# Moving a block transpose's transfers to SyncE and letting another planner order the body, in a hybrid mLSTM and DeltaNet decoder block

## The chip, the cores and the metric

The kernel runs on one core of a Trainium2 chip. A core has TensorE (matmul), VectorE, ScalarE, GpSimd and SyncE, each with its own queue of instructions that it works off in order, and 16 DMA engines that all queues share. SyncE and ScalarE issue the transfers here. The metric is the device time of one execution in microseconds; beside it stands the span of the profiled execution, from its first to its last recorded instruction.

## The reference

One layer over 512 tokens of width 2048, in float32:

```
u    = rmsnorm(x, norm_w)
proj = u @ w_in                                  # some 20,500 columns
mLSTM branch (8 heads, q and k of 128, v of 256):
    chunkwise matrix memory with exponential input gate, sigmoid forget gate, running maximum
    h_a = rmsnorm(h_a) * ml_norm_w * sigmoid(ml_o) * silu(ml_z)
DeltaNet branch (16 heads of 128):
    q, k, v = silu(causal conv of width 4); q, k L2-normalised
    delta rule in chunked WY form: (I + tril(b k k^T decay, -1)) sol = rhs, then a recurrence
    h_b = rmsnorm(h_b, dn_norm_w) * silu(dn_z)
y    = sigmoid(gate_a) * (h_a @ w_out[:2048]) + sigmoid(gate_b) * (h_b @ w_out[2048:])
out  = rmsnorm(x + y, final_norm_w)
```

The kernel uses chunks of 128 tokens, which gives the same function.

## The kernel before

**Products.** The float32 products are made of three fp32r products each: a weight tile `wr` (256 KB, loaded by SyncE at L146) is split into a rounded part `wh` (ScalarE, `split_hi`, L113) and a rest `wl` (VectorE, `split_lo`, L116), and `u` was split in the same way into `uh` and `ul`. `proj_cm` (L212 to L214) makes 256 columns with the channels on the partitions, `proj_wide` (L242 to L244) 512 columns with the tokens on the partitions. Each of the 768 weight tiles feeds twelve matmuls of 128x512. There are four raw buffers (`NRAW`), four pairs of split ones (`NSPL`), and loads are written down up to four tiles ahead of use (`RAHEAD`), splits three (`SAHEAD`).

**Units and steps.** The body goes through twelve units, in rounds of one mLSTM unit (two heads) and two DeltaNet units (two heads each). A unit makes its projections one after the other, and its other work runs as generators beside the projections of later units: `start(gen, wait)` puts one on a list, and `tick()`, called after every six matmuls of a projection, moves each one on whose waiting steps are over. `yield n` means: go on n steps later. So a step is six matmuls.

**A DeltaNet unit.** `dn_front_k` forms k k^T and solves the 32x32 diagonal blocks of the triangular system by substitution on VectorE: 31 pairs of small operations on `tmp` and `xi` (L553, L555). The result goes to DRAM and back in another layout (`xd`, then `tt`, both issued by SyncE), and VectorE transposes `tt` to `tn` (L565). `dn_front_q` makes q k^T (`pqk`, L573), which needs the convolved q in `kq` (L440 to L447: ScalarE copies the projection out of its bank, VectorE convolves, ScalarE takes a tanh, VectorE finishes at L447). `dn_back` (L602 to L636) joins the blocks to the full inverse and uses `tn` and `tt`; `dn_chain` runs the recurrence over four chunks.

**Turned tiles.** `turn` transposes a tile of 128 x (4 x 128) values: VectorE transposes its 32x32 blocks (L468), and `travel` brings the blocks to their places through DRAM, with four writes of 64 KB (L476), one for each quarter of the partitions, and one read of 256 KB (L478). This is done 72 times: for k of the mLSTM heads (`kw`), q (`qn`) and v (`vt`) of the DeltaNet heads, and the normalised results of both (`mhn`, `os`). After a result was turned, `gated` multiplies it with its gate on VectorE and stores it to `h_d` (L482 to L484); it is started `TURN` steps after the turn.

**What sets the order.** TensorE's instructions stay in the order in which they are written (`manual_schedule` for PE). [...] Weight loads and splits are moved forward by `2 * PRIO`, evictions under `urgent()` by `PRIO`, and the four writes under `urgent(2)` by `2 * PRIO`; the read is not moved. [...]

After the units come the merge gates' projections (tanh of them goes to `tg_d`), then the output projection (L937 to L939) with the loads of `h_d`, and the final norm.

Of the kernel before, what the change touches and what calls it, by code (L numbers as in the profile page):

```python
# [17 lines left out]
NC = S // P  # L18
# [8 lines left out]
GNARROW = 4  # L27
GLAG = 3
KLAST = 4
TURN = 9  # L30
KWAIT, QWAIT = 4, 8
EPS = 1e-6
CAP = 15.0
# [6 lines left out]
BS = 32  # L40
# [5 lines left out]


@with_exitstack
def hybrid_block(
    ctx: ExitStack,  # L50
    tc: tile.TileContext,
    x: bass.AP,
# [13 lines left out]
    nc = tc.nc  # L66
# [102 lines left out]
    def urgent(level=1):  # L169
        return tc.high_priority(offset=level * PRIO)  # L170
# [4 lines left out]
    def start(gen, wait=0):  # L175
        active.append([gen, clock["t"] + wait])
# [251 lines left out]
    def row_bcast(r, name):  # L428
        t = wk.tile([P, NC, P], F32, tag="rb", name=name, bufs=3)
        nc.sync.dma_start(t.rearrange("p c t -> p (c t)"), rows_d[r, :].partition_broadcast(P))  # L430
        return t

    def bc(col, n):
        return col.unsqueeze(2).to_broadcast([P, NC, n])
# [22 lines left out]
    def token_norms(pk, dst):  # L457

        jk = wk.tile([P, P], F32, tag="jk", name="njk", bufs=1)
        for c in range(NC):  # L460
            with urgent():
                A.activation(jk, pk[:, c, :], AF.Square, accum_out=dst[:, c:c + 1])

    def turn(src, dst):


        o = dst if dst is not src else wk.tile([P, NC, P], F32, tag="to", name="to", bufs=2)
        V.transpose(o if len(src.shape) == 3 else o.rearrange("p n c -> p (n c)"), src)  # L468
        start(travel(o, dst), 1)

    def travel(o, dst):
        d = dr.tile([16, BS, 4, BS], F32, tag="td", name="td", bufs=8)
        ov = o.rearrange("p n (j c) -> p (n j) c", c=BS)
        with urgent(2):
            for a in range(4):
                nc.scalar.dma_start(d[:, :, a, :].rearrange("m r c -> r m c"), ov[a * BS:(a + 1) * BS])  # L476
        yield 3
        nc.scalar.dma_start(dst, d.rearrange("(n j) r a c -> (j r) n (a c)", n=NC))  # L478
        yield 1

    def gated(hn, w, g, kt):
        V.scalar_tensor_tensor(out=g, in0=hn.rearrange("p c t -> p (c t)"), scalar=w, in1=g, op0=ALU.mult,  # L482
                               op1=ALU.mult)
        nc.sync.dma_start(h_d[kt], g)  # L484
        yield 1

    def dn_front_k(hs, kq, u):
        for j in range(2):
            h = hs[j]
            rb = row_bcast(16 + h, "gb")  # L490
            dm = wk.tile([P, NC, P], F32, tag="dm", name="dm")
            G.affine_select(out=dm, in_=rb, pattern=[[0, NC], [1, P]], channel_multiplier=-1, base=0,
                            compare_op=ALU.is_ge, fill=-1e30)
            A.activation(rb, rb, AF.Exp)
            ge = wk.tile([P, NC], F32, tag="ge", name="ge", bufs=4)
            V.tensor_copy(ge, rb[:, :, P - 1])
            for c in range(NC):
                A.activation(dm[:, c, :], dm[:, c, :], AF.Exp, bias=ngam[:, c, h:h + 1])
            u["dm"].append((dm, rb, ge))
        nk = wk.tile([P, 2, NC], F32, tag="nk", name="nk")  # L500
        cs = wk.tile([P, 2, NC], F32, tag="cs", name="cs")
        for j in range(2):
            pk = psw.tile([P, NC, P], F32, tag="wk", name="pkt")
            for c in range(NC):
                T.transpose(pk[:, c, :], kq[j][:, 0, c * P:(c + 1) * P], ident)
            token_norms(pk, nk[:, j, :])
            ke = wk.tile([P, NC, P], F32, tag="ke", name="ke", bufs=4)
            with urgent():
                A.copy(ke, pk)
            u["ke"].append(ke)  # L510
            yield 1
        V.tensor_scalar(out=nk, in0=nk, scalar1=EPS, scalar2=None, op0=ALU.add)
        V.reciprocal(cs, nk)
        for j in range(2):
            V.tensor_tensor(out=cs[:, j, :], in0=cs[:, j, :], in1=beta[:, :, hs[j]], op=ALU.mult)
        u["nk"] = nk

        for j in range(2):
            dm, eg, ge = u["dm"][j]
            G.tensor_tensor(out=dm, in0=dm, in1=bc(cs[:, j, :], P), op=ALU.mult)  # L520
            ke = u["ke"][j]
            G.tensor_tensor(out=ke, in0=ke, in1=bc(dm[:, :, P - 1], P), op=ALU.mult)
        G.tensor_tensor(out=nk, in0=nk, in1=half, op=ALU.pow)
        yield 3
        ld = dr.tile([2 * NC, 4, BS, BS], F32, tag="ld", name="ld", bufs=2)
        for j in range(2):
            aq = wk.tile([P, NC, 2, P], F32, tag="aq", name="aq", bufs=4)
            u["aq"].append(aq)
            pk = psw.tile([P, NC, P], F32, tag="wk", name="pk")
            for c in range(NC):  # L530
                tsl = slice(c * P, (c + 1) * P)
                T.matmul(pk[:, c, :], kq[j][:, 0, tsl], kq[j][:, 0, tsl], start=True, stop=True)
            with urgent():
                V.tensor_tensor(out=aq[:, :, 0, :], in0=pk, in1=u["dm"][j][0], op=ALU.mult)
            for b in range(4):
                bs = slice(b * BS, (b + 1) * BS)
                nc.sync.dma_start(ld[j * NC:(j + 1) * NC, b, :, :].rearrange("c s t -> s c t"), aq[bs, :, 0, bs])
            yield 1


        ls = wk.tile([P, BS, BS], F32, tag="ls", name="ls", bufs=1)
        for q in range(4):
            nc.sync.dma_start(ls[q * NSYS:(q + 1) * NSYS], ld.rearrange("g b s t -> (g b) s t"))
        xi = wk.tile([P, BS // 4, BS], F32, tag="xi", name="xi", bufs=1)
        G.memset(xi, 0.0)
        for q in range(4):
            G.memset(xi.rearrange("p m t -> p (m t)")[q * NSYS:(q + 1) * NSYS, q:(BS // 4) * BS:BS + 4], 1.0)
        yield 4
        for i in range(BS - 1):
            n, m = BS - 1 - i, i // 4 + 1  # L550
            tmp = wk.tile([P, 80], F32, tag="tmp", name="tmp")
            tv = tmp[:, 0:n * m].rearrange("p (a b) -> p a b", b=n)
            V.tensor_tensor(out=tv, in0=ls[:, i, i + 1:BS].unsqueeze(1).to_broadcast([P, m, n]),  # L553
                            in1=xi[:, 0:m, i].unsqueeze(2).to_broadcast([P, m, n]), op=ALU.mult)
            V.tensor_tensor(out=xi[:, 0:m, i + 1:BS], in0=xi[:, 0:m, i + 1:BS], in1=tv, op=ALU.subtract)  # L555
            if i % 2:
                yield 1
        xd = dr.tile([2 * NC, 4, BS // 4, 4, BS], F32, tag="xd", name="xd", bufs=2)
        tt = wk.tile([P, 2 * NC, BS], F32, tag="tt", name="tt", bufs=1)
        tn = wk.tile([P, 2 * NC, BS], F32, tag="tn", name="tn", bufs=1)  # L560
        with urgent():
            for q in range(4):
                nc.sync.dma_start(xd[:, :, :, q, :].rearrange("g b m t -> (g b) m t"), xi[q * NSYS:(q + 1) * NSYS])
            nc.sync.dma_start(tt, xd.rearrange("g b m q t -> (b m q) g t"))
            V.transpose(tn.rearrange("p g m -> p (g m)"), tt.rearrange("p g t -> p (g t)"))  # L565
        u.update(tn=tn, tt=tt)

# [72 lines left out]
    def dn_chain(j, hs, kq, u):  # L640
# [50 lines left out]
        with urgent():  # L691
            V.tensor_tensor(out=os_, in0=po, in1=bc(rsd, P), op=ALU.mult)
        turn(os_, os_)
        start(gated(os_, normc[:, 32:33], u["g"][j], KT + h), TURN)

# [100 lines left out]
    def ml_fin(j, hs, u):  # L796
        h = hs[j]
        hm = u["hm"][j]
        for i in range(2):
            hn = wk.tile([P, NC, P], F32, tag="os", name="mhn")  # L800
            turn(hm[i], hn)
            kt = 2 * h + i
            start(gated(hn, normc[:, 16 + kt:17 + kt], u["g"][j][i], kt), TURN)
            yield 1
# [168 lines left out]
        nc.sync.dma_start(out[c * P:(c + 1) * P, HD:D], hf[:, c, HD:D])  # L973


# [1 line left out]
_INS = ["x", "norm_w", "w_in", "ml_i_bias", "ml_f_bias", "ml_norm_w", "dn_conv_w",  # L977
        "dn_a_log", "dn_dt_bias", "dn_norm_w", "w_out", "final_norm_w"]
# [20 lines left out]
```

## Time and profile before

| | |
|---|---|
| median of 3 runs | 2459.25 us (2456.11 to 2459.51) |
| profiled execution, its own time | 2458.59 us |
| its span | 2456.8 us |
| mean granted TensorE clock | 0.978 |
| TensorE busy | 2328.6 us, 95% |
| VectorE busy | 1130.9 us, 46% |
| ScalarE busy | 819.9 us, 33%, issuing transfers not counted |
| transfers issued by ScalarE, all kinds | 363 |
| transfers issued by SyncE | 1103 |
| HBM read and written | 260.58 and 42.01 MB |

In the profile PE is TensorE's matmul side and PEld its weight loads, DVE is VectorE, ACT ScalarE, POOL GpSimd and SP SyncE; ACTq and SPq are what those two queues issue. L476 is line 476 of the kernel. `td<-to` means that `td` is written from `to`. A wait "A <- B" is idle time of A's engine ended by B. Busy shares are averages over stages; what one wait is worth is read where it occurs.

### The profile page before, as it was taken

What the parts mean: (1) busy time and instruction counts of PE and PEld (TensorE: products, weight loads), DVE (VectorE), ACT (ScalarE), POOL (GpSimd) and SP (SyncE); (2) the same over time, 40 slices, a digit from 0 to 9 for tenths busy, and PEclk for the clock granted to TensorE, in tenths of its full rate; (3) what the DMA queues carried; (4) which work ended last, traced back from release to release, by engine and by line L of the source; (5) the groups of instructions that cost most, each with busy time, mean ns of one, the idle gap of its engine ahead of it and who ended that gap; (6) DMA issues with size and microseconds to landing.
All of it is one profiled execution on the core that took longest, in us unless ns stands there. A gap on an engine that the chain in (4) does not pass through costs nothing.

```text
span 2456.8 us, 32123 instructions
## 1 busy us (share of the span) xinstructions
PE 2328.6 (95%) x11711; PEld 1941.0 (79%) x11711; DVE 1130.9 (46%) x2187; ACT 819.9 (33%) x1846; POOL 192.6 (8%) x261
## 2 busy tenths in 40 slices
PE   7999987999998799999989999988999999999998
PEld 5888776888877687887768788776998888888886
DVE  5533756433375643238463324747333322433434
ACT  5333342332434233243423324342233322422222
POOL 0000202000020200002020001101000000010010
PEclk9999998999999899999989999998999999999999
DMA  4433544453354445335454533544475443643433
GB/s 146 130 99 96 125 126 113 121 132 95 99 127 121 123 112 133 95 95 136 115 130 108 129 95 96 128 114 114 112 218 168 136 145 112 198 129 115 131 113 128
DMA packets 423199, 304.71 MB, mean 124 GB/s; under 512 B 200065, under 2 KB 362082, under 8 KB 423042
## 3 DMA queue, kind: packets, MB, share of 16 engines
q1 hardware_dynamic: 232898, 264.84, 37.6%
q10 hardware_dynamic: 190144, 37.84, 7.8%
q8 instruction: 91, 1.49, 0.2%
q14 instruction: 66, 0.54, 0.1%
HBM read 260.58 MB, written 42.01 MB: 123 GB/s over the span
## 4 chain that ended last, share of the span: by engine, by line
PE 81%; DVE 9%; DMA 3%; ACTq 2%; issue 2%; ACT 1%; POOL 1%; SPq 0%; DVEq 0%; POOLq 0%
PE pj L212 13%; PE pj L214 13%; PE pj L213 13%; PE py L939 5%; PE py L937 5%; PE py L938 5%; PE pg L243 4%; PE pg L242 4%; PE pg L244 4%; PE pv L242 2%; PE pv L244 2%; PE pv L243 2%; ACTq L476 2%; DVE tmp L553 2%; DVE wl L116 2%; DVE xi L555 2%
## 5 line engine op out<-in xcount | busy, mean ns | idle before, releaser
L116 DVE TENSOR_TENSOR wl<-wr,wh 128x512 fp32r<-128x512 f32 x768 | 533.2, 702 | 949.4 <-ACT wh L113 934.9
L113 ACT CAST wh<-wr 128x512 fp32r<-128x512 f32 x768 | 472.0, 621 | 1357.1 <-PE pj L213 518.9
L212 PE MATMUL pj<-uh,wh 128*128 128x512 f32 x1792 | 739.7, 413 | 32.7 <-ACT thz L454 26.2
L214 PE MATMUL pj<-uh,wl 128*128 128x512 f32 x1792 | 708.6, 395 | 3.8 <-DVE wl L116 3.8
L213 PE MATMUL pj<-ul,wh 128*128 128x512 f32 x1792 | 708.2, 395 | 0.0
L212 PEld LDWEIGHTS pj<-uh,wh 128*128 128x128 f32 x1792 | 343.4, 192 | 102.5 <-ACT thz L454 27.9
L214 PEld LDWEIGHTS pj<-uh,wl 128*128 128x128 f32 x1792 | 341.8, 191 | 82.0 <-DVE wl L116 6.9
L213 PEld LDWEIGHTS pj<-ul,wh 128*128 128x128 f32 x1792 | 343.2, 192 | 64.5
L937 PE MATMUL py<-wh,hh 128*128 128x512 f32 x512 | 199.2, 389 | 0.0
L938 PE MATMUL py<-wl,hh 128*128 128x512 f32 x512 | 199.2, 389 | 0.0
L939 PE MATMUL py<-wh,hl 128*128 128x512 f32 x512 | 199.2, 389 | 0.0
L242 PE MATMUL pg<-wh,uh 128*128 128x512 f32 x384 | 149.4, 389 | 0.0
L243 PE MATMUL pg<-wl,uh 128*128 128x512 f32 x384 | 149.4, 389 | 0.0
L244 PE MATMUL pg<-wh,ul 128*128 128x512 f32 x384 | 149.4, 389 | 0.0
L938 PEld LDWEIGHTS py<-wl,hh 128*128 128x128 f32 x512 | 96.1, 188 | 20.1
L939 PEld LDWEIGHTS py<-wh,hl 128*128 128x128 f32 x512 | 96.1, 188 | 20.0
L937 PEld LDWEIGHTS py<-wh,hh 128*128 128x128 f32 x512 | 96.1, 188 | 19.8
L242 PE MATMUL pv<-wh,uh 128*128 128x512 f32 x256 | 99.6, 389 | 0.0
L243 PE MATMUL pv<-wl,uh 128*128 128x512 f32 x256 | 99.6, 389 | 0.0
L244 PE MATMUL pv<-wh,ul 128*128 128x512 f32 x256 | 99.6, 389 | 0.0
L242 PEld LDWEIGHTS pg<-wh,uh 128*128 128x128 f32 x384 | 72.1, 188 | 15.1
L244 PEld LDWEIGHTS pg<-wh,ul 128*128 128x128 f32 x384 | 72.1, 188 | 15.0
(244 smaller groups left out, 2348.6 us busy)
## 6 DMA issues: line engine op xcount, KB each, us to landing
wr<-in_w_in_dram SPq DMA_DIRECT2D x640, 256.0 KB, 2.8
wr<-in_w_out_dram SPq DMA_DIRECT2D x128, 256.0 KB, 3.0
td<-to ACTq DMA_DIRECT2D x128, 64.0 KB, 2.1
hr<-h_d SPq DMA_DIRECT2D x32, 256.0 KB, 3.6
tgl<-tg_d SPq DMA_DIRECT2D x32, 256.0 KB, 3.1
tg_d<-tgw SPq DMA_DIRECT2D x24, 256.0 KB, 3.7
xt<-in_x_dram SPq DMA_DIRECT2D x8, 512.0 KB, 8.6
gb<-rows_d SPq DMA_DIRECT2D x16, 256.0 KB, 3.9
```

Source lines behind the costliest of these rows:

```text
L113: A.copy(hi, src)
L116: V.tensor_tensor(out=lo, in0=src, in1=hi.bitcast(F32), op=ALU.subtract)
L212: T.matmul(ps[j], hi[:, k, wsl], uh[:, kt, :], start=(kt == 0), stop=False)
L213: T.matmul(ps[j], hi[:, k, wsl], ul[:, kt, :], start=False, stop=False)
L214: T.matmul(ps[j], lo[:, k, wsl], uh[:, kt, :], start=False, stop=(kt == KT - 1))
L242: T.matmul(ps[c], uh[:, kt, tsl], hi[:, 0, :], start=(kt == 0), stop=False)
L243: T.matmul(ps[c], uh[:, kt, tsl], lo[:, 0, :], start=False, stop=False)
L244: T.matmul(ps[c], ul[:, kt, tsl], hi[:, 0, :], start=False, stop=(kt == KT - 1))
L476: nc.scalar.dma_start(d[:, :, a, :].rearrange("m r c -> r m c"), ov[a * BS:(a + 1) * BS])
L937: T.matmul(ps[c], hh[base][:, kt, tsl], hi[:, 0, :], start=(kt == 0), stop=False)
L938: T.matmul(ps[c], hh[base][:, kt, tsl], lo[:, 0, :], start=False, stop=False)
L939: T.matmul(ps[c], hl[base][:, kt, tsl], hi[:, 0, :], start=False, stop=(kt == KT - 1))
```

## The change

Four things change. The transfers of `travel` are issued by SyncE in place of ScalarE. Their steps move: the writes two steps after the turn instead of one, the read four steps after the writes instead of three and with the priority that the writes have, `gated` twelve steps after the turn instead of nine. The VectorE transpose of `tt` to `tn` comes ten steps after its transfers instead of right behind them. And the whole body stands in one `tc.block`, for which the planner takes the framework's timeline simulation as its model of the chip in place of its usual one; so the order of every queue but TensorE's can become another.

```diff
-TURN = 9
+TURN = 12
...
 @with_exitstack
-def hybrid_block(
+def hybrid_body(
...
         V.transpose(o if len(src.shape) == 3 else o.rearrange("p n c -> p (n c)"), src)
-        start(travel(o, dst), 1)
+        start(travel(o, dst), 2)
...
         with urgent(2):
             for a in range(4):
-                nc.scalar.dma_start(d[:, :, a, :].rearrange("m r c -> r m c"), ov[a * BS:(a + 1) * BS])
-        yield 3
-        nc.scalar.dma_start(dst, d.rearrange("(n j) r a c -> (j r) n (a c)", n=NC))
+                nc.sync.dma_start(d[:, :, a, :].rearrange("m r c -> r m c"), ov[a * BS:(a + 1) * BS])
+        yield 4
+        with urgent(2):
+            nc.sync.dma_start(dst, d.rearrange("(n j) r a c -> (j r) n (a c)", n=NC))
         yield 1
...
             nc.sync.dma_start(tt, xd.rearrange("g b m q t -> (b m q) g t"))
+        yield 10
+        with urgent():
             V.transpose(tn.rearrange("p g m -> p (g m)"), tt.rearrange("p g t -> p (g t)"))
...
+def hybrid_block(tc, *args):
+    with tc.block(schedule_with_timeline_sim=True):
+        hybrid_body(tc, *args)
```

## The prediction, made before the changed kernel was run

> **What bounds the kernel now.** I read the page's first two parts, then the list of what TensorE waited for, then the timeline around its long waits, and last the clock in short windows and the page's list of DMA queues.
>
> ```profile
> span 2456.8 us, 32123 instructions
> PE 2328.6 (95%) x11711; PEld 1941.0 (79%) x11711; DVE 1130.9 (46%) x2187; ACT 819.9 (33%) x1846; POOL 192.6 (8%) x261
> ...
> PEclk9999998999999899999989999998999999999999
> ```
>
> TensorE is busy for 95%, so at most 2456.8 - 2328.6 = 128.2 us of idle time, and what a low clock adds, can be won. Where it idles (waits in us in total, times, longest):
>
> ```profile
> PE pqk L573 <- DVE kq L447: 62.3, 8, 11.5
> PE pj L212 <- ACT thz L454: 26.2, 4, 7.0
> PE pprm L103 <- DMA nrow<-in_ml_norm_w_dram: 15.3, 1, 15.3
> PE pj L212 <- ACT wh L113: 5.4, 4, 1.9
> PE pj L214 <- DVE wl L116: 3.8, 3, 1.6
> ```
>
> The 15.3 us are the start, which the change leaves alone. The other four rows, with one wait of 1.1 us on a convolution input, are 98.8 us in the body. They come in rounds of one mLSTM and two DeltaNet units, four rounds in all: each has a short pqk wait (4.1 to 4.4 us), a thz wait (6.1 to 7.0) and a long pqk wait (11.1 to 11.5). Round one in the timeline (start, length, engine, and in brackets the idle time before and what ended it):
>
> ```profile
> 321.53 1.98 ACTq L476 DMA_DIRECT2D td<-to  x4
> ...
> 323.55 5.03 ACTq L476 DMA_DIRECT2D td<-mhn  x8
> 328.62 0.62 ACT L113 CAST wh<-wr 128x512 fp32r<-128x512 f32 x1 [9.04 <-DMA td<-mhn]
> ...
> 330.27 0.79 PE L212 MATMUL pj<-uh,wh 128*128 128x512 f32 x1 [7.05 <-ACT thz L454]
> ...
> 402.63 0.63 ACT L446 ACTIVATE th<-kq 128x512 f32<-128x512 f32 x1
> ...
> 413.61 0.68 DVE L447 SCALAR_TENSOR_TENSOR kq<-th,kq 128x512 f32<-128x512 f32 x1
> ...
> 414.35 2.08 PE L573 MATMUL pqk<-kq 128*128 128x128 f32 x8 [11.55 <-DVE kq L447]
> ...
> 425.22 1.66 ACT L113 CAST wh<-wr 128x512 fp32r<-128x512 f32 x3 [18.06 <-DMA td<-to]
> 428.21 0.45 DVE L565 STREAM_TRANSPOSE tn<-tt 128x256 f32<-128x256 f32 x1 [7.48 <-DMA tt<-xd]
> ```
>
> At 321.5 ScalarE issues twelve writes of turned tiles, from 321.53 to 328.58, and stands 9 us before its next cast; the evictions that free TensorE's banks are behind them. That is the thz wait. At 402.63 the tanh that kq needs starts, so kq could run at 403.3; VectorE's order puts the substitution pairs (L553, L555) first, and kq runs at 413.6. That is the long pqk wait, and it is a matter of order alone.
>
> After a wait TensorE also runs slowly (columns: stretch, its length, PE busy and matmuls, granted clock, DMA share, GB/s):
>
> ```profile
> 331.00:332.00 1.00, 1.00 (x4) 0.50 1.05 309
> ...
> 334.00:336.00 2.00, 2.00 (x11) 1.00 0.69 179
> ```
>
> At clock 0.50 matmuls start 0.43 us apart, at 1.00 0.23. The slow stretch after the return lasts about 3.4 us after a short pqk, 3.6 after a thz and 4.9 after a long pqk wait; half of that is lost: 1.7, 1.8 and 2.4 us.
>
> **The change, part by part.** Round by round, all that waits cost is 62.3 + 4 x (1.7 + 2.4) = 78.7 us for pqk, 26.2 + 4 x 1.8 = 33.4 for thz, 10.3 for the small ones: 122.4. With none of them and nothing new the span would be 2334.
>
> *ScalarE loses the transfers.* 72 turned tiles, each four writes and a read:
>
> ```profile
> L476 ACTq DMA_DIRECT2D td<-to x128: 309/516/1819, 312.3 to 1799.2; - x128
> ...
> L478 ACTq DMA_DIRECT2D mhn<-td x16: 366/383/460, 268.3 to 1615.2; - x16
> ```
>
> 288 writes at 0.51 us and 72 reads at 0.38 us are 147 + 27 = 174 us of ScalarE's queue. Most lay beside matmuls. On the path are the bursts: the four thz waits (33.4 us), and the four waits for a cast (5.4), of which the one at 521.7 follows a burst of 16 writes (511.45 to 521.02). With the writes gone ScalarE goes on to its cast and eviction as soon as the matmuls end, so I take both as won: 38.8 us. Late next would be the banks themselves, at their ordinary 0.6 us evictions. The bounds are 0 (SyncE's burst then stops the weights instead) and 38.8.
>
> *SyncE gains them.* Its 1103 issues take 422 us (summed over its row in the trace) and get 174 more: 596 of 2457. The length is no issue; the place is. Behind a turned tile's write or read on SyncE stand weight loads, the reads of broadcast rows and the h stores; for the weight loads wait ScalarE's cast, VectorE's subtraction and then TensorE. A write now waits for VectorE's transpose, a read for its writes to land (2.1 us median for a write). The cover is the lead of the weights: pairing the n-th load with the n-th tile's first matmul in the trace gives a median of 17.7 us (one in a hundred under 9.7), which agrees with up to four raw and three split tiles ahead of the one in use, 2.72 us each. A burst of twelve writes is 7 us, a wait for landing some 2 us: under the cover. So I cost it at 0; without the cover each such burst would cost up to its 7 us. The long end is ScalarE's stand of 18.06 us above, which is as long as the lead: if SyncE stood so, nothing would be left.
>
> Weight loads and turned tiles have used different rings so far:
>
> ```profile
> q1 hardware_dynamic: 232898, 264.84, 37.6%
> q10 hardware_dynamic: 190144, 37.84, 7.8%
> ```
>
> 7.8% of the span over 72 tiles is 2.7 us of all 16 engines for each tile. Behind one on the same ring a weight load would land in 2.8 + 2.7 = 5.5 us, behind three in 11. The first is well under the lead and the second is not, if SyncE's own stand is added. [...]
>
> *Four steps to the read, two to the writes, TURN 12.* A step is six matmuls, 6 x 0.227 = 1.36 us. Writes come one step later, the read two steps later (1 + 3 steps after the turn, 5.4 us, become 2 + 4, 8.2 us), and the gated product six steps after the read in place of five. VectorE's waits for these reads (vt 15.6, gz 7.4, mg 2.3 us in total) ended no TensorE wait, so 0; tiles are held some 4 us longer, which only a full buffer would show. The read becomes urgent as well, so that it may pass weight loads on SyncE: 0.38 us each, in the cover.
>
> *The transpose of tt waits ten steps.* Now VectorE stands 41.4 us in eight waits for tt. Behind it are weight subtractions; the three waits for wl (3.8 us, one at 429.28 just after the transpose at 428.21) come of it. Gain 3.8. tn is first used 31 us after it was made (304.9 and 336.3), ten steps are 13.6 us, so nobody waits for it: 0; if that cover went, TensorE would wait at L602.
>
> *The order is made anew.* One block ordered by another time model: every order but TensorE's, which is written out, can change. The trace can't show the new one. It can win the 78.7 us of pqk waits, by putting kq before the substitution, or lose: a further group of matmuls in each DeltaNet unit that waits as the long pqk does would cost 8 x (11.4 + 2.4) = 110 us. I take half of the pqk time, 39 us: the four short ones of the eight show the same work at a third of the price, and the tanh of the long one stood 2.3 us behind the turned tiles' writes (its input ended at 400.3), which are gone from that queue. Against it I set new waits of 3 us a round, between the small ones (0.6 to 1.9) and the short pqk: 12 us. Entering and leaving a block is not in the trace; bounds are 0 and 5 us (some twice the longest unexplained stretch in the chain, 2.2 us near the end), taken 1, by the 1.8 us that lie around the span.
>
> Sum: 2456.8 - 38.8 - 3.8 - 39 + 12 + 1 = 2388 for the span. The profiled execution took 2458.6 for its 2456.8, and the median of the runs is 2459.25: add 2.4, so 2391. Within 0.2% (5 us) is what a measurement of this kernel can't tell from no change.
>
> **The rivals.** *Only ScalarE's relief counts*: the new order is as good as the old, and the pqk waits stay. 2459 - 38.8 - 3.8 + 1 = 2418. For it: kq's lateness is VectorE's own affair. Against: the order is made afresh by other times, so that it stays equal would be chance.
>
> *SyncE's line stops the weights*: a write waits there for a late VectorE transpose, loads stand behind it and behind the small packets. ScalarE's waits for td are 138 us in 20 places (61.8 + 65.7 + 6.7 + 3.9); if half of it came through, 69, plus 20 us of slow clock in as many places, less the 42.6 won: 2459 + 69 + 20 - 42.6 = 2505. It decides when SyncE's stand and the landing together pass the lead of 17.7 us. Against it: SyncE waits 1390 us for VectorE to free a raw tile, so it is mostly idle.
>
> *The new order makes another group late*, the case on the other side with one place: a product of the DeltaNet units whose VectorE input is put behind the substitution as kq is. 2459 + 110 - 42.6 + 1 = 2527. From 42 us in total, that is 5 us a unit, it outweighs what ScalarE's relief gives.
>
> *No difference*: thz and casts are held up by other work of ScalarE, and the order comes out alike: 2459.
>
> **How the numbers follow.** Forecast 0.50 (its own range 2340 to 2425: from nearly all 122 us won, to new waits of 45 in place of 12), ScalarE's relief alone 0.15, no difference 0.04, SyncE's line 0.11, the order worse 0.20. Faster 0.65, same 0.04, slower 0.31. The low end, 2340, is just above 2337, all waits gone. The high end, 2510, takes in half of SyncE's line and a third of the bad order (which spreads from 2470 to 2600); left out are 0.05 + 0.13 above and 0.01 below.
>
> **What would show it.** Right: no wait of L212 for thz; td issues in SyncE's row; no ScalarE cast that waits for td; tn without a wait for tt; fewer and shorter pqk waits; ScalarE's busy time unchanged at 820. Wrong: casts that wait for wr landings, TensorE waiting for wh or wl (SyncE's line), or a new row of TensorE waits for a VectorE or ScalarE result of more than 40 us in total (the order), with more 0.50 in the clock.

## The result and the profile after

The changed kernel takes 2416.0 us (median of 4 runs, 2413.2 to 2416.8) beside 2457.7 us before: a ratio of 0.9829 (95% interval 0.9812 to 0.9846). That is 41.7 us faster, where 68 had been forecast (2459 to 2391). The top of its page:

```profile
span 2415.0 us, 32146 instructions
## 1 busy us (share of the span) xinstructions
PE 2318.6 (96%) x11711; PEld 1934.3 (80%) x11711; DVE 1112.4 (46%) x2187; ACT 828.4 (34%) x1846; POOL 188.0 (8%) x261
...
q1 hardware_dynamic: 422978, 302.62, 46.1%
```

The span fell by 41.8 us. TensorE's busy time fell by 10.0 us (2328.6 to 2318.6) for the same 11711 matmuls, because less of it ran at the low clock (mean 0.978, now 0.986). Its idle time fell by 31.8 us (128.2 to 96.4). All turned tiles now travel on SyncE's ring, q1, which carries 302.62 MB in place of 264.84. What TensorE waited for in the changed kernel (total, times, longest):

```profile
PE p L605 <- DVE tn L568: 40.1, 7, 9.9
PE pprm L103 <- DMA nrow<-in_ml_norm_w_dram: 15.8, 1, 15.8
PE pj L212 <- ACT yp L440: 13.0, 8, 4.0
PE pnum L768 <- DVE c L778: 5.9, 4, 1.8
PE put L291 <- DVE xt L284: 5.6, 1, 5.6
PE pj L212 <- ACT thz L454: 4.2, 3, 2.3
PE pqk L576 <- DVE kq L447: 0.4, 1, 0.4
```

The list is turned over. The pqk wait is gone (62.3 us before, 0.4 now), and so, nearly, is the thz wait (26.2, now 4.2) and that for `wh` (5.4, now none). In their place stands a wait that the old profile did not have at all: the first matmuls of `dn_back` (L605) wait 40.1 us for `tn`, seven times in eight units. In the body all waits together were 98.8 us and are 63.6; at the start 4 us were lost (15.3 + 2.1 before, 15.8 + 5.6 now).

The chain to the first of the `tn` waits, from the timeline of all engines in the changed kernel:

```profile
324.01 0.69 DVE L639 TENSOR_TENSOR vt<-vt,nk 128x512 f32<-128x512 f32 x1 [2.71 <-DMA vt<-td]
...
324.82 0.17 DVE L556 TENSOR_TENSOR xi<-xi,tmp 128x8 f32<-128x8 f32 x1
...
326.65 1.01 SPq L146 DMA_DIRECT2D wr<-in_w_in_dram  x2
327.70 2.63 SPq L564 DMA_DIRECT2D xd<-xi  x4
...
332.87 0.37 SPq L565 DMA_DIRECT2D tt<-xd  x1
...
336.07 0.45 DVE L568 STREAM_TRANSPOSE tn<-tt 128x256 f32<-128x256 f32 x1 [2.89 <-DMA tt<-xd]
```

The last pair of the substitution is done at 325.0, having stood on VectorE behind a product that waited 2.7 us for a turned tile; SyncE then issues weight loads and two reads of turned tiles before `xd`, which goes out 2.7 us later (so in every other unit; in the rest, and before the change, `xd` goes out at once); `xd` and `tt` take until 336.0, and `tn` follows at once. Before the change the same unit had its last pair at 297.4 and `tn` at 304.9. The step from the first pair to the last is what grew: 24.0 us on average over the eight units before, 48.8 after. Why, a stretch of VectorE's row in the changed kernel shows:

```profile
302.55 0.22 DVE L556 TENSOR_TENSOR xi<-xi,tmp 128x66 f32<-128x66 f32 x1
302.68 0.75 DVE L443 SCALAR_TENSOR_TENSOR vt<-yp,convc,vt 128x512 f32<-128x512 f32 x1
303.35 0.21 DVE L554 TENSOR_TENSOR tmp<-ls,xi 128x60 f32<-128x60 f32 x1
303.48 0.68 DVE L116 TENSOR_TENSOR wl<-wr,wh 128x512 fp32r<-128x512 f32 x1
304.08 0.75 DVE L443 SCALAR_TENSOR_TENSOR vt<-yp,convc,vt 128x512 f32<-128x512 f32 x1
304.74 0.21 DVE L556 TENSOR_TENSOR xi<-xi,tmp 128x60 f32<-128x60 f32 x1
```

The small operations depend on each other, and the new order lays one or two operations of 0.7 us between them. Counted in the traces, a unit's substitution had 12.5 other VectorE operations inside it before and has 51.0 now. Of the 24.8 us by which it grew 5.9 are waits of VectorE inside it, nearly all for turned tiles (0.3 us a unit before, 6.2 now); the rest is the work laid between. `pqk` was freed by where `kq` now stands: of the 62 small operations 25 or 44 stood ahead of the second `kq` of q before, 3 or 13 now.

### The profile page after: what moved, and what is told of

Its sections match the earlier page's. It is cut to its first block, busy times and chain, and to the rows that moved or that the text cites. A ratio compares the mean times of both kernels' runs of the same rounds, so it can differ in the third digit from the quotient of the medians.

```text
span 2415.0 us, 32146 instructions
## 1 busy us (share of the span) xinstructions
PE 2318.6 (96%) x11711; PEld 1934.3 (80%) x11711; DVE 1112.4 (46%) x2187; ACT 828.4 (34%) x1846; POOL 188.0 (8%) x261
## 3 DMA queue, kind: packets, MB, share of 16 engines
q1 hardware_dynamic: 422978, 302.62, 46.1%
## 4 chain that ended last, share of the span: by engine, by line
PE 81%; DMA 6%; DVE 5%; SPq 4%; ACT 2%; issue 1%; POOL 0%; DVEq 0%; POOLq 0%; ACTq 0%
PE pj L212 13%; PE pj L213 13%; PE pj L214 13%; PE py L940 5%; PE py L942 5%; PE py L941 5%; PE pg L243 4%; PE pg L244 4%; PE pg L242 4%; SPq L476 2%; PE pv L243 2%; PE pv L242 2%; PE pv L244 2%; PE pjt L227 1%; PE pjt L229 1%
## 5 line engine op out<-in xcount | busy, mean ns | idle before, releaser
L116 DVE TENSOR_TENSOR wl<-wr,wh 128x512 fp32r<-128x512 f32 x768 | 539.8, 705 | 879.8 <-ACT wh L113 870.0
L243 PEld LDWEIGHTS pg<-wl,uh 128*128 128x128 f32 x384 | 72.1, 188 | 15.0
```

The source lines that it names most:

```text
L116: V.tensor_tensor(out=lo, in0=src, in1=hi.bitcast(F32), op=ALU.subtract)
L243: T.matmul(ps[c], uh[:, kt, tsl], lo[:, 0, :], start=False, stop=False)
```

## The experiments

Three suspects were to be told apart for the new wait: the new order (which draws out the substitution), SyncE's line (which issues `xd`, `tt` and the turned tiles late), and the ten steps. And the gain had to be divided between the new order and the move to SyncE.

### The parts alone

The order alone is the kernel before with the block around its body.

```diff
-def hybrid_block(
+def hybrid_body(
...
+def hybrid_block(tc, *args):
+    with tc.block(schedule_with_timeline_sim=True):
+        hybrid_body(tc, *args)
```

> The kernel before with its body in the block that is ordered by the timeline simulation; transfers, steps and the transpose of tt stay as before. Theory (the new order removes the pqk waits by putting kq ahead of the substitution, and pays with a late tn, because the substitution is drawn out on VectorE): pqk waits under 5 us in total, substitution some 45 us long in place of 22 to 26, tn waits of 30 to 45 us, thz waits kept at 15 to 30 as ScalarE still issues the bursts; time 2415 to 2440. Rival A (tn is late because SyncE's line holds the xd and tt transfers behind the turned tiles): tn waits under 10 us, time near 2400. Rival B (the ten steps make tn late): the same, tn waits under 10 us.

Measured 2405.5 us, ratio 0.9792 (0.9777 to 0.9806): faster than the whole change. Its waits of TensorE:

```profile
PE p L602 <- DVE tn L565: 18.4, 6, 5.5
...
PE pj L212 <- ACT thz L454: 14.5, 7, 3.8
PE pj L212 <- ACT wh L113: 12.7, 6, 3.0
...
PE pqk L573 <- DVE kq L447: 0.6, 1, 0.6
```

So the order alone takes away the pqk wait and brings the `tn` wait, as the theory had it, with a substitution of 46.9 us. But there are only 18 us of `tn` waits in place of 30 to 45, and the time is under the range given: something else in the change makes `tn` later and costs time.

The rest of the change without the block:

```diff
-def hybrid_block(tc, *args):
-    with tc.block(schedule_with_timeline_sim=True):
-        hybrid_body(tc, *args)
```

> The changed kernel without the block, so with the order of the usual planner: SyncE issues the turned tiles, with the new steps and the ten steps for tn. Theory: thz waits and casts behind td writes gone (under 5 us), pqk waits kept at 40 to 62 us, substitution 22 to 26 us long and no tn wait; time 2415 to 2430. Rival A (SyncE's line): tn waits of 20 us or more here too. Rival B (ten steps): tn waits here too.

Measured 2550.0 us, ratio 1.0382 (1.0367 to 1.0398), so 93 us slower than before, where 27 to 42 faster was expected. TensorE's waits in it (total, times, longest):

```profile
PE p L605 <- DVE tn L568: 81.0, 8, 16.7
PE pj L212 <- ACT wh L113: 45.1, 8, 10.2
PE pj L212 <- ACT thz L454: 39.4, 4, 10.6
...
PE pqk L576 <- DVE kq L447: 4.7, 4, 1.2
```

SyncE's row of the timeline around the first substitution in the same run (start, us, what it issued, how many):

```profile
285.60 0.46 SPq L544 DMA_DIRECT2D ls<-ld  x1
297.80 3.44 SPq L146 DMA_DIRECT2D wr<-in_w_in_dram  x4
301.49 6.47 SPq L476 DMA_DIRECT2D td<-to  x8
...
319.24 2.80 SPq L146 DMA_DIRECT2D wr<-in_w_in_dram  x3
322.09 1.40 SPq L544 DMA_DIRECT2D ls<-ld  x3
```

One of the four reads of `ls` is issued at 285.6; the other three stand behind weight loads, the next of which goes out 12 us later, and behind sixteen writes of turned tiles, until 322.1. The substitution starts at 327 and `tn` comes at 351. So it is in four of the eight units. In the other four the reads are in time, but the `xd` writes go out 14 to 26 us after the last pair, with weight loads before them, and `tn` starts 31 to 33 us after it (6.5 to 7.9 before). ScalarE, too, stood longer for weights (casts that waited for `wr`: 69.4 us, 30.9 before). SyncE's line is late here, as in the rival of that name, but the transfers that stand in it to TensorE's cost are the substitution's own, which the rival did not name; the next run shows how much of the time they are.

The list shows another thing that was not expected: the pqk waits are 4.7 us in place of 62.3, under the usual planner. Given other steps and another issuer, it too lays down another order: 0 or 10 of the small operations stand ahead of the second `kq` of q here. So the block is not the only way to free `kq`.

To see whether the place in SyncE's line is the cause, the small transfers were moved forward:

```diff
-                nc.sync.dma_start(ld[j * NC:(j + 1) * NC, b, :, :].rearrange("c s t -> s c t"), aq[bs, :, 0, bs])
+                with urgent(2):
+                    nc.sync.dma_start(ld[j * NC:(j + 1) * NC, b, :, :].rearrange("c s t -> s c t"), aq[bs, :, 0, bs])
...
-            nc.sync.dma_start(ls[q * NSYS:(q + 1) * NSYS], ld.rearrange("g b s t -> (g b) s t"))
+            with urgent(2):
+                nc.sync.dma_start(ls[q * NSYS:(q + 1) * NSYS], ld.rearrange("g b s t -> (g b) s t"))
...
-        with urgent():
+        with urgent(2):
             for q in range(4):
                 nc.sync.dma_start(xd[:, :, :, q, :].rearrange("g b m t -> (g b) m t"), xi[q * NSYS:(q + 1) * NSYS])
```

> The run e2_sync_alone (the change without the new order) with the small transfers of the substitution (ld, ls, xd, tt) moved forward in the priority as far as the weight loads and the turned tiles. Theory (in e2 the three ls reads stand on SyncE behind weight loads that wait for a free buffer and behind sixteen writes, so that the substitution starts 41 us after the first of them): first ls read to first substitution pair under 12 us, tn waits under 20 us in place of 81, time 2430 to 2490. Rival (the lateness is not one of SyncE's order): tn waits stay over 50 us, time over 2520.

Measured 2463.3 us, ratio 1.0022 (1.0013 to 1.0031). The first `ls` read is 6.1 us ahead of the first pair, and the `tn` wait is gone from the list of TensorE's waits:

```profile
PE pj L212 <- ACT wh L113: 55.6, 15, 10.2
PE pj L214 <- DVE wl L116: 33.1, 7, 6.7
...
PE pqk L578 <- DVE kq L447: 4.7, 4, 1.2
```

So 87 of the 93 us hung on where a few small transfers stand on SyncE. What is left are 88.7 us of waits for `wh` and `wl`. Casts still wait 53.2 us for `wr`, but the longest of TensorE's waits are not late weights. Of the waits for `wh` four of about 10 us make up 39.7; before the first of them ScalarE's row shows

```profile
424.44 0.63 ACT L446 ACTIVATE th<-vt 128x512 f32<-128x512 f32 x1 [3.61 <-DVE vt L443]
...
427.00 1.12 ACT L113 CAST wh<-wr 128x512 fp32r<-128x512 f32 x2
```

The weight tile of that cast had landed at 419.3; the cast stood behind a tanh whose input VectorE made between pairs of the substitution, and behind the squares of q that follow it. Of the waits for `wl` four of 6.2 to 6.7 us make up 25.3, and in these the subtraction comes 7.7 us after its cast, behind an unbroken stretch of the substitution. So under the usual planner the rest of the change wins nothing even so: the pqk waits have gone, and others have taken over, 65 us of them from where the substitution stands on VectorE.

The converse: the whole change with ScalarE issuing the turned tiles again.

```diff
-                nc.sync.dma_start(d[:, :, a, :].rearrange("m r c -> r m c"), ov[a * BS:(a + 1) * BS])
+                nc.scalar.dma_start(d[:, :, a, :].rearrange("m r c -> r m c"), ov[a * BS:(a + 1) * BS])
...
-            nc.sync.dma_start(dst, d.rearrange("(n j) r a c -> (j r) n (a c)", n=NC))
+            nc.scalar.dma_start(dst, d.rearrange("(n j) r a c -> (j r) n (a c)", n=NC))
```

> The changed kernel with the turned tiles' transfers issued by ScalarE again, all else kept (steps, block, ten steps). Theory: tn waits stay at 30 us or more, as the substitution is still drawn out; thz waits come back with the bursts, 10 to 30 us; time 2425 to 2450. Rival A (SyncE's line): tn waits fall under 15 us; time under 2410.

Measured 2403.9 us, ratio 0.9783 (0.9768 to 0.9797). TensorE's waits in this run:

```profile
PE pj L212 <- ACT wh L113: 23.1, 7, 5.9
PE pj L212 <- ACT thz L454: 17.8, 4, 5.2
```

There is no `tn` wait in this list, against the theory, which wanted 30 us or more; rival A had it right. The bursts on ScalarE are back with 40.9 us of waits, and still the kernel is 12 us faster than the changed one. So SyncE's part in the changed kernel swaps 41 us of waits for `thz` and `wh` against 59 of others (`tn` 40.1, `yp` 13.0, `pnum` 5.9). With the new order alone, which differs from this run in the steps, the time was the same (2405.5), with 18.4 us of `tn` waits: where ScalarE issues, the steps are worth nothing that can be told from zero.

The block itself, with the usual planner, which lays down the same order as before:

```diff
-    with tc.block(schedule_with_timeline_sim=True):
+    with tc.block():
```

> The kernel before in a plain block with the usual planner; every queue has the same instructions in the same order as before. This prices entering and leaving the block: theory 0 to 5 us, so 2457 to 2462.

Measured 2458.5 us over 10 runs, ratio 1.0003 (0.9994 to 1.0013): no cost that can be told from zero.

### What makes tn late

First the substitution itself, moved forward in the priority:

```diff
-            V.tensor_tensor(out=tv, in0=ls[:, i, i + 1:BS].unsqueeze(1).to_broadcast([P, m, n]),
+            with urgent():
+                V.tensor_tensor(out=tv, in0=ls[:, i, i + 1:BS].unsqueeze(1).to_broadcast([P, m, n]),
...
-            V.tensor_tensor(out=xi[:, 0:m, i + 1:BS], in0=xi[:, 0:m, i + 1:BS], in1=tv, op=ALU.subtract)
+                V.tensor_tensor(out=xi[:, 0:m, i + 1:BS], in0=xi[:, 0:m, i + 1:BS], in1=tv, op=ALU.subtract)
```

> The changed kernel with the 31 pairs of the substitution moved forward in the planner's priority as the evictions are. Theory (tn is late because the new order draws the substitution out on VectorE, 48 us in place of 24): substitution under 35 us, tn waits under 10 us; but kq falls behind it again, so pqk waits come back, 20 to 60 us; time 2400 to 2440. Rival (tn is late because SyncE's line is late with the transfers): tn waits stay over 25 us.

Measured 2417.0 us, ratio 0.9834 (0.9815 to 0.9853), with `tn` waits of 39.5 us. VectorE's order came out the same to the last instruction, so neither theory was tested, and the 1.0 us to the changed kernel is scatter. It does show that priority as high as that of the evictions does not pull the substitution together in this kernel; why was not tested.

Then SyncE's line, by letting ScalarE issue only `xd` and `tt`:

```diff
-                nc.sync.dma_start(xd[:, :, :, q, :].rearrange("g b m t -> (g b) m t"), xi[q * NSYS:(q + 1) * NSYS])
-            nc.sync.dma_start(tt, xd.rearrange("g b m q t -> (b m q) g t"))
+                nc.scalar.dma_start(xd[:, :, :, q, :].rearrange("g b m t -> (g b) m t"), xi[q * NSYS:(q + 1) * NSYS])
+            nc.scalar.dma_start(tt, xd.rearrange("g b m q t -> (b m q) g t"))
```

> The changed kernel with only the transfers of the solved blocks (four xd writes and the tt read of each DeltaNet unit) issued by ScalarE, past SyncE's line. Theory A (the xd writes stand behind turned tiles and weight loads on SyncE, 2.7 us in every other unit): tn waits fall from 40 to under 20 us, time near 2395. Theory B (VectorE is late with the substitution itself, because it stands for the reads of turned tiles that SyncE issues late): tn waits stay over 25 us, time 2410 to 2420.

Measured 2412.9 us, ratio 0.9819 (0.9802 to 0.9836), not to be told from the changed kernel. `tn` is no longer waited for, but another wait has taken all of it, as the list of TensorE's waits in this run shows:

```profile
PE pj L212 <- ACT thz L454: 33.2, 9, 6.9
...
PE pj L212 <- ACT yp L440: 13.8, 8, 3.7
```

By the waits theory A holds, by the time theory B. Both miss the point: ScalarE's queue now stands for the end of the substitution (8.5 us before its cast at 325.2 in the first unit), TensorE loses the time at `thz`, ahead of L605, and by then `tn` is there. From the first `ls` read to `tn` takes 62 to 65 us in this run, 61 to 66 in the changed kernel, 59 to 62 with ScalarE issuing, 37 to 45 before the change. In the runs so far a wait that goes at one place comes back at the next, and this path is longer than TensorE's own way to L605.

The ten steps, taken back:

```diff
-        yield 10
-        with urgent():
             V.transpose(tn.rearrange("p g m -> p (g m)"), tt.rearrange("p g t -> p (g t)"))
```

> The changed kernel with the transpose of tt written right behind its transfers, as before the change. Theory (the ten steps do not make tn late, since it starts as soon as tt lands): tn waits 35 to 55 us, time 2410 to 2430. Rival (the ten steps hold tn back): tn waits under 20 us, time 2385 to 2400.

Measured 2419.9 us, ratio 0.9848 (0.9832 to 0.9864), `tn` waits of 40.1 us. The ten steps do not make `tn` late. In the traces every queue has the same instructions in the same order in this run as in the changed kernel, so under the new planner the ten steps change nothing at all, and the 3.9 us between the two are scatter from one measurement to the next. The other steps, put back as they were:

```diff
-TURN = 12
+TURN = 9
...
-        start(travel(o, dst), 2)
+        start(travel(o, dst), 1)
...
-        yield 4
-        with urgent(2):
-            nc.sync.dma_start(dst, d.rearrange("(n j) r a c -> (j r) n (a c)", n=NC))
+        yield 3
+        nc.sync.dma_start(dst, d.rearrange("(n j) r a c -> (j r) n (a c)", n=NC))
```

> The changed kernel with the steps of the turned tiles as before (writes one step after the turn, read three steps after them without priority, TURN 9); SyncE still issues, the order is still the new one. Theory (steps and priority of the read are worth nothing by themselves): 2410 to 2422. Rival (on SyncE the later steps are what keeps its line moving): over 2430, with more waits of ScalarE for weight loads.

Measured 2423.8 us, ratio 0.9862 (0.9845 to 0.9878), with `tn` waits of 53.8 us, just above the theory's range. The steps and the read's priority are worth some 8 us beside the changed kernel, but 4 beside the run without the ten steps, which has the changed kernel's order: the edge of what these runs can tell.

### Giving the path its time

If the path to `tn` is too long for its place, the place can be moved: the back part, whose first matmuls are L605, starts eight steps (11 us) later.

```diff
-        start(dn_back(hs, kq, u), 4)
+        start(dn_back(hs, kq, u), 12)
```

> The changed kernel with the start of the DeltaNet units' back part (whose first matmuls wait for tn) twelve steps after the Z projection in place of four, so 8 x 1.36 = 11 us later. Both theories: tn waits under 8 us, as the longest was 9.9; theory: nothing else takes their place and the time is 2365 to 2385. Rival: the recurrence, now 11 us later, delays the next round's buffers, and the time stays at 2405 to 2420.

Measured 2348.1 us (2347.3 to 2349.2), ratio 0.9554 (0.954 to 0.9569), beyond the theory's best: 110 us under the kernel before and 68 under the changed one. The top of its page:

```profile
span 2346.6 us, 32173 instructions
## 1 busy us (share of the span) xinstructions
PE 2300.0 (98%) x11711; PEld 1921.5 (82%) x11711; DVE 1110.4 (47%) x2187; ACT 829.2 (35%) x1846; POOL 186.9 (8%) x261
```

And what TensorE still waited for in it:

```profile
PE pprm L103 <- DMA nrow<-in_ml_norm_w_dram: 15.3, 1, 15.3
PE pnum L768 <- DVE c L778: 5.7, 4, 1.6
PE put L291 <- DVE xt L284: 5.5, 1, 5.5
PE pj L214 <- DVE wl L116: 5.5, 4, 2.1
PE pj L212 <- ACT yp L440: 3.0, 5, 0.6
```

`tn` is there 3.5 to 12.1 us ahead of L605, and nothing has taken the wait's place; that of `yp` went down too (in the changed kernel the longest, at 421.3, follows the squares of q at L462, the other work at the head of the back part, which stood 5.4 us for a turned q). Idle time fell by 49.8 us against the changed kernel (96.4 to 46.6). Busy time fell by another 18.6 (2318.6 to 2300.0) for the same 11711 matmuls: with the long waits gone the granted clock has a mean of 0.998, where the changed kernel has 0.986.

The same with ScalarE issuing, which prices SyncE's part where `tn` no longer hides it (the edit is that of the run e4_scalar_issues with the one above):

> The changed kernel with the back part twelve steps after the Z projection, and with the turned tiles issued by ScalarE again: the run e7_back_later with the issuer alone undone. Theory (SyncE's part is worth the bursts on ScalarE, hidden so far because any time won there was given back as waiting for tn): thz and wh waits of 25 to 45 us here, none of tn; time 2375 to 2395, so SyncE's part is worth some 38 us beside e7's 2348. Rival (SyncE's part brings nothing under the new order either way): within 8 us of 2348.

Measured 2369.7 us, ratio 0.9641 (0.9627 to 0.9655): the theory holds in kind, but SyncE's part is worth 21.6 us and not 38. Of the 19.0 us between the two spans 12.0 are idle time and 7.0 slower matmuls (mean clock 0.993 in place of 0.998). Back in TensorE's list are the waits of the bursts, 19.0 us in place of the 25 to 45 expected; against them stand smaller waits that went (`wl` 5.5 us, `pnum` 2.9):

```profile
PE pj L212 <- ACT thz L454: 19.0, 4, 6.1
```

And the same shift on the kernel before:

> The kernel before with the back part twelve steps after the Z projection in place of four, nothing else. Theory (in the old order tn is there 28 us ahead of its use, so that the shift has nothing to win, and the pqk and thz waits stay): 2445 to 2470. Rival (the shift wins by itself, whatever the order): under 2430.

Measured 2416.6 us, ratio 0.9833 (0.9818 to 0.9847), so the theory is wrong and the rival right: the shift gains 42 us by itself, as much as the whole change. TensorE's waits in this run:

```profile
PE pj L212 <- ACT thz L454: 30.7, 7, 7.4
PE pqk L573 <- DVE kq L447: 16.7, 4, 4.4
```

The four long pqk waits are gone and the four short ones are left: 26 of the small operations now stand ahead of the second `kq` in those units, in place of 44. What the edit moves is the back part and the recurrence of the unit before, some of whose VectorE and ScalarE work fell between the two convolutions of q; with another step count it falls elsewhere. That this is what pushed `kq` back is read from the traces, and which of its operations did it was not tested. With the runs without the block this makes three edits that each freed the long pqk waits.

| turned tiles issued by | usual planner, back part at 4 | at 12 | new planner, at 4 | at 12 |
|---|---|---|---|---|
| ScalarE | 2457.7 | 2416.6 | 2403.9 | 2369.7 |
| SyncE | 2550.0 | not run | 2416.0 | 2348.1 |

The two runs with ScalarE and the usual planner have the old steps, all others the new ones; and each program has its own order, so a step from row to row is the issuer together with the order that the planner then lays down.

## Why the prediction was right, and where it was not

The direction and the range (2340 to 2510) held. The forecast of 2391 was 25 us too low, and that it came this near is in part luck: two large errors in its sum, one each way, cancel for the most part. The time alone would have spoken for the rival "Only ScalarE's relief counts" (2418), which the waits refute, since the pqk waits that it keeps are gone.

*The order made anew* was sized at half of the pqk time; all of it went (62.3 to 0.4 us), through the mechanism named: `kq` ahead of all but 3 or 13 of the substitution's operations. The order alone is worth 52 us, more than the whole change. But the rest of the change without the block frees `kq` as well (4.7 us), so the new planner is enough for this and not needed for it.

*The transpose of tt* is the step that failed. "Nobody waits for it: 0" took the 31 us between `tn` and its use (28 to 32 over the eight units) for granted while the order was to be laid down anew. The cover went, and TensorE waits at L605, the place that the text named for that case. The ten steps had no part in it, and none in the gain of 3.8 that the term gave them: the waits for `wl` are gone with and without them. The mechanism is that of the rival "another group late", in the very units and behind the very substitution, but inverted: not a product put behind the substitution, but the substitution drawn out by what was put between. At 40.1 us it stayed just under the 42 at which it would have decided; but it is more than the 40 us that the prediction itself named as the sign of being wrong by the order. In place of the 12 us allowed for new waits, the body had 59.0 (`tn`, `yp`, `pnum`).

*ScalarE's relief* was right in the rows and wrong in the sum. Of the 31.6 us of `thz` and `wh` waits 27.4 went. But the 38.8 us were not won: they were given back as waiting for `tn`, since TensorE only came to L605 earlier. With the back part later, so that `tn` is in time, the move is worth 21.6 us, not 38.8: there the bursts on ScalarE cost only 19.0 us of `thz` waits and none for `wh`, where both together were 31.6 before and 27.2 with the order alone.

*SyncE's gain at 0* was the other wrong step. The lead of the weights held, as argued: its median is 17.7 us in the changed kernel too, and TensorE's list has no wait for `wh` or `wl`. But the lead covers weights alone. VectorE stood 26 us for reads of turned tiles before and stands 91 now (`mhn` 35.2, `vt` 23.6, `os` 16.5, `kw` 15.4), part of it inside the substitution. Most of this came with the new order: it is 63 with the order alone and 66 when ScalarE issues, and under the usual planner with SyncE issuing only 7. By itself such a stand decides nothing: it is 97 in the fastest run, where the path has its time. The prediction did ask who waits behind the writes, but listed weight loads, broadcast rows and h stores, and left out `ld`, `ls`, `xd` and `tt`; 87 of the 93 us lost without the block hung on these. In the changed kernel, where the path to `tn` has no time to spare, the move costs 12 us.

*The shared ring.* The prediction's estimate, from 2.8 us for a load's landing and 2.7 us of the DMA engines for a turned tile, was that on one ring with the tiles a weight load lands in 5.5 us behind one of them and in 11 behind three. The median shows no such cost: from issue to landing a weight load takes 2.8 us in both kernels. The longest went from 6.6 to 8.7 us, but was 11.1 with ScalarE issuing in the new order, so the runs do not tie it to the shared ring.

*The steps* were costed at 0 and are worth 4 to 8 us, at the edge of what the runs can tell; *the block* at 1, and is 0 within the interval. *The start*, which was taken as left alone, lost 4 us, 3.5 of them in the wait for `xt`, which is 5.5 to 5.7 us in every run with the new planner and 1.9 to 2.1 in every run with the usual one.

*The other signs.* Not all that the prediction wanted to see came: 4.2 us of waits for `thz` are left, and `tn` still waits for `tt`, 28.5 us on VectorE in place of 41.4. One sign of being wrong came in a weak form: casts wait 56.8 us for `wr` in place of 30.9, but TensorE does not wait for them.

## What to carry to other kernels

Before costing a relief on one engine, follow each path that meets the bottleneck's fixed order and note how much slack it has there; time won ahead of a path with no slack was only waited for later here. When an order is laid down anew, no cover read from the old trace should be counted as zero cost: the 28 to 32 us of cover here became a wait of up to 9.9. Any edit of the program can bring another order, under the usual planner too, so look at the order of each run before giving its gain to the edit: two edits here left every queue as it was. And when a wait moves from place to place under several edits, the fixed place may be what is wrong: one number, the start of the back part, was worth 68 us here.

## What the hardware showed that was not expected

Putting 190,000 small packets (q10's 190144 before, 64 now) on the weight loads' ring did not change their median landing (2.8 us), and a 64 KB write took SyncE as long to issue as ScalarE (medians of 0.50 and 0.51 us). What differed in these runs is who stands behind. And the low clock after waits adds to their price more than the prediction counted: it set 23.6 us of slow clock beside 88.5 us of pqk and thz waits, about 0.27 us for each; from the changed kernel to the one with the later back part 49.8 us of idle time went, and 18.6 us of slower matmuls with it (mean clock 0.986, then 0.998), about 0.37 for each.
